# A hybrid decoder trunk whose program is ordered by the list scheduler's time-line model instead of its default model

## The chip, the cores and the metric

The kernel runs on one core of one Trainium2 chip. The metric is device time in microseconds (us), lower is better. Two numbers are used throughout: the time of a run, and the span of one profiled execution, from its first instruction to its last. A core has five engines that work side by side: PE (TensorE, matmuls and transposes; PEld is its weight load), DVE (VectorE), ACT (ScalarE), POOL (GpSimd) and SP (SyncE, which here only issues DMAs). Each engine takes its instructions strictly in the order in which the program lists them for that engine, and waits at semaphores for the others. So the order of the list, engine by engine, is part of the program.

## The reference

The input is x, 1024 tokens of 1024 channels, float32, and two layers of weights. One layer computes, in the reference's own words cut short:

```python
h = rmsnorm(x, norm_gain)
proj = h @ w_in          # split into gq,gk,gv,gb,ga,gz, mq,mkv,mkr,mz, lx,lz
o_a = rmsnorm(gated_delta_rule(q, k, v, g, beta), gdn_out_norm) * silu(gz)  # 4 heads
o_b = causal_block_attention(qf, kf, vm) * silu(mz)                         # 8 heads
o_c = rg_lru(causal_dwconv(lx) + b, ...) * silu(lz)                         # 512 channels
x = x + concat([o_a, o_b, o_c]) @ w_out
```

q, k and v of the first mixer go through a width-4 causal convolution and SiLU. The gated delta rule runs in 16 chunks of 64 tokens, and each chunk needs the state S that the one before it left:

```python
v_new = u_n - w_n @ state
o = (q_n * exp(g_n)) @ state + a_n @ v_new
state = state * exp(g_last) + k_scaled.T @ v_new
```

u_n and w_n come from the inverse of a unit lower triangular 64x64 matrix for each chunk and head. After the second layer a last RMS norm follows.

## The kernel before, in words

**Layout.** Everything is kept transposed: 128 channels on the partitions, 1024 tokens along the row. Every large product is done as three matmuls on a split of both operands into a coarse half and a rest (`mm3`, lines 121 to 123: hi times hi, lo times hi, hi times lo). `load_w` brings one 128-column block of weights: line 104 is the DMA into `wst`, line 109 (ACT) or 111 (DVE) casts it to `whi`, line 112 (POOL) subtracts to get `wlo`.

**The filler.** `in_tile` computes one 128-channel tile of the input projection: 48 matmuls of 512 columns into a two-bank PSUM buffer called `pbig`. There are two such buffers, so the third tile in a row waits until somebody has read the first one out. One layer has 38 such tiles. Names in the listings below carry the tile's number: `pbig_2519` is one tile.

**The chain.** The delta rule handles its four heads as two pairs, "pair 0" and "pair 1", one after the other in each layer. For each pair:

- `gdn_tok` and `gdn_pre` (lines 313 to 367) make the small matrices; the last matmuls are line 367.
- `gdn_inverse` sends the matrices through DRAM into another shape (lines 383, 393, 394) and inverts all of them at once with 60 dependent DVE instructions, `itmp<-inv` and `inv<-inv,itmp`, and one COPY (line 391).
- `gdn_prep`, once for each quarter q of the tokens, loads the inverse back (lines 401 and 403, tiles `mt` and `tq`) and runs four groups of matmuls (lines 415, 421, 426, 434) with DVE steps between them (`z`, `tf`).
- `gdn_scan`, also by quarters, runs the 16 steps of the recurrence. A step is: line 459 on PE (four 128-column matmuls, `pssc<-S,wq`), `vn` on DVE, line 463 on PE (`pssc<-vn,kd`), and the new state `S` on DVE (two instructions), which the next step's line 459 reads. Every second step adds line 471 (`pspr<-vn,at`) for the output.
- `gdn_norm` scales and transposes the outputs: squares on ACT, `ms`, 16 scalings of `at` on POOL (line 95), 16 transposes on PE (line 496), four `gzh` on DVE, each with loads and stores of SP.

After pair 1 the RG-LRU mixer (`lru`) takes four tiles of its own (`lx`: `pbig_3924`, `pbig_4020`, `pbig_4116`, `pbig_4212` in the first layer), convolves each into `u` on ACT and DVE, and goes on with gates and a scan along the row. Then come the first half of the output projection (`pspr`, 384 matmuls), the attention of eight heads and the second half of the output projection. Line 797 transposes the attention's weights, lines 808 and 810 multiply them with the values, line 747 makes scores.

**What sets the order.** The Python code only emits instructions with a priority number. A list scheduler then runs over the whole program and a model of the machine: whenever an engine of the model is free, it takes, among the instructions whose inputs the model has ready, the one with the best priority number. The result is one fixed list for each engine. Three things in the code steer it. The tiles' matmuls are emitted with 20000 added to their priority number, so that they come behind everything else that is ready; the instructions that empty a tile's PSUM buffer and that cast weights are emitted with 20000 taken off; and the place in the code at which a tile is emitted gives its base number:

```python
LOW = 20000
with self.prio(self.LOW):       # in in_tile: the 48 matmuls of a tile
with self.prio(-self.LOW):      # in load_w: cast and subtract; also conv, silu, squares
FILL = ((1, 1, 2, 0, 1), (1, 0, 3, 0, 2))   # tiles emitted between the chain's steps
```

So "filler" is not pinned to a place: the scheduler puts tile matmuls wherever its model of the machine sees PE free and nothing of better priority ready. What the model takes an instruction to last therefore decides where the filler lands. The change touches `kernel()` alone, at the line that opens the context in which all instructions are emitted and ordered.

## Time and profile before

| | before |
|---|---|
| runs, us | 2186.76, 2194.24, 2195.37; median 2194.24 |
| profiled execution, us | 2189.71 |
| its span, us | 2187.9 |
| mean granted TensorE clock | 0.985 |
| PE busy | 2079.0 us, 95% of the span |
| DVE, ACT, POOL busy | 1318.7, 881.4, 705.6 us |
| DMA, mean busy share of 16 engines | 31% |

The profile counts an engine as busy while an instruction of it runs; matmuls are pipelined, so the busy time of PE says that something is in flight, not that it goes at its peak. The work between two rows of one kind is better read from the distance of their starts. In the rows of a timeline the first number is the start in us from the beginning of the span, the second the length in us, then come engine, line, operation, output<-inputs, sizes, and in brackets how long the engine had been idle and what released it.

The two layers run the same code; in the first, the scan of pair 0 lies at about 244 to 306 us, the inverse of pair 1 at 365 to 441, the scan of pair 1 at 441 to 502, its norm at 502 to 517, the attention at 716 to 1045.

### The profile page before, as it was taken

To read this page: it belongs to the slowest core of one execution; us is meant where nothing else is said; L and a number is where in the kernel's file an instruction comes from. 1 tells how busy PE (TensorE), PEld (TensorE's weight loads), DVE (VectorE), ACT (ScalarE), POOL (GpSimd) and SP (SyncE) were. 2 spreads that over 40 slices of the span, in tenths; PEclk is the share of its full clock that TensorE was granted. 3 is DMA by queue.
4 is the path that set the end of the run, shared out by engine and by line. 5 is a ranking of instruction groups with operands and counts; after the bars stand their busy time and mean duration, and the time that the engine had idled before them with its cause. 6 is when DMAs were issued, how large, how long until landed. Compare 5 with 4: busy or idle time off the path is not lost. (4 is left out here: it accounts for less than half of the span.)

```text
span 2187.9 us, 28714 instructions
## 1 busy us (share of the span) xinstructions
PE 2079.0 (95%) x10380; PEld 1691.9 (77%) x10380; DVE 1318.7 (60%) x2496; ACT 881.4 (40%) x1788; POOL 705.6 (32%) x712
## 2 busy tenths in 40 slices
PE   7999999999989999999989999999998999999997
PEld 3788877787778788888668888787876778888874
DVE  6546555644751777776665475474458337776766
ACT  5251235134820453544542413531366115554534
POOL 3222322233452333332142213232236333332322
PEclk9999999999999999999999999999999999999999
DMA  4223212322153115244421331134122530335172
GB/s 141 78 79 101 73 44 87 101 92 90 54 181 116 61 31 193 81 146 157 160 88 49 93 101 44 58 103 139 49 80 94 188 102 27 100 124 165 61 233 98
DMA packets 135101, 222.06 MB, mean 101 GB/s; under 512 B 37808, under 2 KB 60336, under 8 KB 134960
## 3 DMA queue, kind: packets, MB, share of 16 engines
q1 hardware_dynamic: 134960, 220.24, 31.1%
q8 instruction: 82, 1.34, 0.3%
q14 instruction: 59, 0.48, 0.1%
HBM read 147.31 MB, written 72.88 MB: 101 GB/s over the span
## 5 line engine op out<-in xcount | busy, mean ns | idle before, releaser
L112 POOL TENSOR_TENSOR wlo<-wst,whi 128x1024 fp32r<-128x1024 f32 (+3 forms) x196 | 316.6, 1616 | 869.4 <-DVE whi L111 317.2
L121 PE MATMUL pbig<-h,whi 128*128 128x512 f32 x1216 | 486.6, 400 | 8.3 <-ACT h L127 5.3
L123 PE MATMUL pbig<-h,wlo 128*128 128x512 f32 x1216 | 485.8, 400 | 4.0 <-POOL wlo L112 4.0
L122 PE MATMUL pbig<-h,whi 128*128 128x512 f32 x1216 | 486.5, 400 | 3.2 <-POOL h L128 1.6
L121 PEld LDWEIGHTS pbig<-h,whi 128*128 128x128 f32 x1216 | 231.7, 191 | 56.6 <-ACT h L127 6.6
L122 PEld LDWEIGHTS pbig<-h,whi 128*128 128x128 f32 x1216 | 231.4, 190 | 52.2 <-DVE h L128 4.4
L123 PEld LDWEIGHTS pbig<-h,wlo 128*128 128x128 f32 x1216 | 231.6, 190 | 51.3 <-POOL wlo L112 5.3
L86 ACT ACTIVATE P<-pS,mx,scq 128x512 f32<-128x512 f32 (+1 forms) x192 | 128.1, 670 | 155.9 <-DVE mx L89 83.0
L111 DVE CAST whi<-wst 128x1024 fp32r<-128x1024 f32 x92 | 77.2, 840 | 154.1 <-PE pbig L122 121.9
L95 POOL TENSOR_SCALAR P<-P,mx 128x128 f32<-128x128 f32 (+6 forms) x112 | 80.7, 721 | 215.9 <-DVE mx L768 132.2
L109 ACT CAST whi<-wst 128x256 fp32r<-128x256 f32 (+2 forms) x104 | 46.2, 446 | 202.7 <-DMA wst<-in_w_uq 110.2
L127 ACT CAST pth<-pstp 128x512 fp32r<-128x512 f32 x192 | 91.0, 478 | 74.8 <-PE pstp L797 74.7
L757 DVE TENSOR_REDUCE mx<-pS 128x1 f32<-128x512 f32 (+1 forms) x192 | 106.4, 554 | 16.4 <-PE pS L751 9.7
L128 DVE TENSOR_TENSOR ptl<-pstp,pth 128x512 fp32r<-128x512 f32 x192 | 104.8, 552 | 15.0 <-ACT pth L127 13.8
L86 ACT ACT_TABLE_LOAD x81 | 103.9, 1283 | 3.0 <-PE pssc L123 0.8
L797 PE MATMUL pstp<-con,P 128*128 128x128 f32 x576 | 98.1, 275 | 5.8 <-DVE P L772 5.0
L92 DVE TENSOR_TENSOR xt<-pspj,xt 128x512 f32<-128x512 f32 x96 | 66.2, 690 | 49.5 <-PE pspj L123 26.6
L797 PEld LDWEIGHTS pstp<-con,P 128*128 128x128 f32 x576 | 71.7, 141 | 25.7 <-DVE P L772 7.3
L121 PE MATMUL pspj<-lh,whi 128*128 128x512 f32 x208 | 84.3, 405 | 6.7 <-DVE k L128 6.0
L123 PE MATMUL pspj<-lh,wlo 128*128 128x512 f32 x208 | 81.7, 393 | 0.5 <-POOL wlo L112 0.5
L808 PE MATMUL pspo<-pth,vh 128*128 128x512 f32 x192 | 79.3, 413 | 2.8 <-ACT pth L127 2.8
L122 PE MATMUL pspj<-ll,whi 128*128 128x512 f32 x208 | 81.6, 392 | 0.0
(268 smaller groups left out, 4542.0 us busy)
## 6 DMA issues: line engine op xcount, KB each, us to landing
wst<-in_w_in SPq DMA_DIRECT2D x76, 512.0 KB, 3.6
x<-xt SPq DMA_DIRECT2D x128, 256.0 KB, 3.4
xt<-x SPq DMA_DIRECT2D x112, 256.0 KB, 3.4
mzd<-z SPq DMA_DIRECT2D x16, 512.0 KB, 3.5
wst<-in_w_o SPq DMA_DIRECT2D x16, 512.0 KB, 3.6
mz<-mzd SPq DMA_DIRECT2D x32, 256.0 KB, 3.0
wst<-in_w_o SPq DMA_DIRECT2D x64, 128.0 KB, 2.1
xk<-x SPq DMA_DIRECT2D x32, 256.0 KB, 4.1
```

The costliest lines, as they stand in the source:

```text
L86: self.nc.scalar.activation(out, in_, func, **kw)
L95: self.nc.gpsimd.tensor_scalar(out, a, s, 1.0, ALU.mult, ALU.mult)
L111: nc.vector.tensor_copy(hi[:, :n], st[:, :n])
L112: (eng or nc.gpsimd).tensor_tensor(lo[:, :n], st[:, :n], hi[:, :n].bitcast(F32), ALU.subtract)
L121: nc.tensor.matmul(out, ah, bh, start=(j == 0), stop=False)
L122: nc.tensor.matmul(out, ah, bl, start=False, stop=False)
L123: nc.tensor.matmul(out, al, bh, start=False, stop=(j == n - 1))
L127: self.nc.scalar.copy(hi, x)
L128: (eng or self.nc.vector).tensor_tensor(lo, x, hi.bitcast(F32), ALU.subtract)
L757: nc.vector.tensor_reduce(mx[:, j : j + 1], S[j], AX.X, ALU.max, negate=True)
L797: nc.tensor.transpose(tp[:, qi * 128 : qi * 128 + 128], P[qi][:, kb * 128 : kb * 128 + 128], self.ident)
L808: nc.tensor.matmul(po[:, w], vh[:, vs], th[:, w], start=(j == 0), stop=False)
```

## The change

`TileContext` is given one more argument. With it the list scheduler asks another model of the machine, its time-line model, when an instruction would be ready and how long it takes. The statements that emit instructions, their number, their shapes, buffers and priorities stay as they are. The order of the instructions on each engine changes, and with it where the semaphore waits stand.

```diff
-    with tile.TileContext(nc) as tc:
+    with tile.TileContext(nc, schedule_with_timeline_sim=True) as tc:
         Trunk(tc, ins, {"y": out}).build()
```

The listings below show three places, all on PE and all in the first layer; the second layer reads the same. x2, x4 and x16 at the end of a row count the same instruction in a row.

**The scan of pair 0.** On PE before, in the middle of the scan (line 459 and 463 are the two halves of a step, `pbig` is filler, 415 and 421 belong to the next quarter's prep):

```order
L463 MATMUL pssc<-vn,kd 128x128 x2
L471 MATMUL pspr<-vn,at 128x128 x2
L121 MATMUL pbig<-h,whi 128x512
L459 MATMUL pssc<-S,wq 128x128 x2
L122 MATMUL pbig<-h,whi 128x512
L123 MATMUL pbig<-h,wlo 128x512
L121 MATMUL pbig<-h,whi 128x512
L122 MATMUL pbig<-h,whi 128x512
L463 MATMUL pssc<-vn,kd 128x128 x2
L123 MATMUL pbig<-h,wlo 128x512
```

And PE of the change, from the scan's second step on:

```order
L459 MATMUL pssc<-S,wq 128x128 x2
L123 MATMUL pbig<-h,wlo 128x512
L463 MATMUL pssc<-vn,kd 128x128 x2
L471 MATMUL pspr<-vn,at 128x128 x2
L459 MATMUL pssc<-S,wq 128x128 x2
L463 MATMUL pssc<-vn,kd 128x128 x2
L459 MATMUL pssc<-S,wq 128x128 x2
L463 MATMUL pssc<-vn,kd 128x128 x2
L471 MATMUL pspr<-vn,at 128x128 x2
L415 MATMUL pspr<-tq,mt 128x128 x4
L459 MATMUL pssc<-S,wq 128x128 x2
```

Before, three or four filler matmuls stand between the halves of every step. In the change 22 and 21 of them stand in the first step, one in the second, and none in the 14 steps after it. In the scan of pair 1 the first half of the steps have about 22 fillers each between their halves, and the last nine steps none.

**From the matrices to the inverse, pair 1.** PE before, around the last matmuls of line 367 (named by `pspr_2705`) and the two matmuls of line 191 that follow:

```order
L367 MATMUL pspr_2705<-wq_2250,kT_1583 128x128
L367 MATMUL pspr_2705<-wq_2407,kT_1798 128x128
L122 MATMUL pbig_2872<-h_115,whi_2868 128x512
L191 MATMUL pspr_2849<-sq_2570,ep_70 128x512
L191 MATMUL pspr_2853<-sq_2570,ep_70 128x512
L123 MATMUL pbig_2872<-h_107,wlo_2869 128x512
```

PE of the change, at the same place:

```order
L367 MATMUL pspr_2705<-wq_2250,kT_1583 128x128
L367 MATMUL pspr_2705<-wq_2407,kT_1798 128x128
L191 MATMUL pspr_2849<-sq_2570,ep_70 128x512
L191 MATMUL pspr_2853<-sq_2570,ep_70 128x512
L121 MATMUL pbig_3145<-h_101,whi_3141 128x512
```

From there to the first line 415, which needs the inverse, PE has 306 filler matmuls before and 156 in the change: the tiles `pbig_2872` and `pbig_2932` are already done when line 367 ends.

**The norm of pair 1.** PE before, after the last line 471 of pair 1 (32 rows of lx tiles stand between it and the first of these):

```order
L123 MATMUL pbig<-h,wlo 128x512
L496 MATMUL pspr<-con,at 128x128 x8
L121 MATMUL pbig<-h,whi 128x512
L122 MATMUL pbig<-h,whi 128x512
L496 MATMUL pspr<-con,at 128x128 x4
L123 MATMUL pbig<-h,wlo 128x512
L121 MATMUL pbig<-h,whi 128x512
L496 MATMUL pspr<-con,at 128x128 x4
```

PE of the change:

```order
L459 MATMUL pssc<-S,wq 128x128 x2
L463 MATMUL pssc<-vn,kd 128x128 x2
L471 MATMUL pspr<-vn,at 128x128 x2
L496 MATMUL pspr<-con,at 128x128 x16
L121 MATMUL pbig<-h,whi 128x512
L122 MATMUL pbig<-h,whi 128x512
```

The first two lx tiles have moved ahead into the scan, so line 496 follows the scan at once, and the filler behind it is the third lx tile, `pbig_4116`, which needs the buffer that `pbig_3924` holds. On DVE, in both kernels, the convolution that empties `pbig_3924` stands behind the four `gzh` of the norm; in the change it is interleaved with that of `pbig_4020`:

```order
L92 TENSOR_TENSOR ms<-ms,rq 128x16
L89 SCALAR_TENSOR_TENSOR gzh<-pspr,onh,gzh 128x512 x4
L939 TENSOR_SCALAR onh<-par 128x1
L89 SCALAR_TENSOR_TENSOR u<-pbig,par,u 128x1023 x2
L89 SCALAR_TENSOR_TENSOR u<-pbig,par,u 128x1022 x2
L89 SCALAR_TENSOR_TENSOR u<-pbig,par,u 128x1021 x2
```

## The prediction, made before the change was run

> **What bounds the kernel now.** I began with the page's first two parts: who is busy, and at which clock.
>
> ```profile
> span 2187.9 us, 28714 instructions
> PE 2079.0 (95%) x10380; PEld 1691.9 (77%) x10380; DVE 1318.7 (60%) x2496; ACT 881.4 (40%) x1788; POOL 705.6 (32%) x712
> PEclk9999999999999999999999999999999999999999
> ```
>
> PE is busy 2079.0 of 2187.9 us, at nearly full clock. It bounds the kernel, and an order can only change the 108.9 us in which PE has nothing in flight, plus the gaps that busy time hides. The second view, PE's waits summed over the run, says where the small ones are; these are its three largest.
>
> ```profile
> PE pspr L121 <- ACT oh L127: 8.0, 2, 4.0
> PE psst L191 <- DVE sq L177: 7.5, 4, 5.7
> PE pspo L810 <- DVE ptl L128: 6.6, 8, 1.5
> ```
>
> No single wait is large. The third view, PE's busy time by stretches of the first layer, shows how that is reached (columns: stretch, its length, PE busy, clock, DMA share, GB/s).
>
> ```profile
> 244.00:306.00 62.00, 61.05 (x377) 1.00 0.12 39
> 365.00:441.00 76.00, 74.69 (x340) 1.00 0.34 106
> 441.00:502.00 61.00, 60.21 (x372) 0.97 0.25 80
> 502.00:517.00 15.00, 14.82 (x65) 1.00 0.41 136
> 716.00:1045.00 329.00, 317.93 (x1726) 1.00 0.35 112
> 1045.00:1133.00 88.00, 78.38 (x323) 0.94 0.38 132
> ```
>
> The first four are the scan of pair 0, the inverse of pair 1, the scan of pair 1 and its norm. In each of them a chain of dependent steps runs over PE, DVE, ACT, POOL and DRAM, and PE idles 1.0, 1.3, 0.8 and 0.2 us, because filler of the input projection stands between the steps. The last two, attention and what follows, idle 11.1 and 9.6 us. So the question for any new order is whether the filler still stands where the chain leaves PE free. The listings answer it: in all four places it does not.
>
> **The scans.** One step of pair 0's scan in the timeline, PE and DVE rows alone; the number behind the start is the length.
>
> ```profile
> 282.09 0.61 PE L459 MATMUL pssc<-S,wq 128*128 128x128 f32 x4
> 282.45 0.48 PE L122 MATMUL pbig<-h,whi 128*128 128x512 f32 x1
> 282.74 0.42 DVE L92 TENSOR_TENSOR vn<-uu,pssc 64x256 f32<-64x256 f32 x1 [2.28 <-PE pssc L459]
> 283.33 0.71 PE L463 MATMUL pssc<-vn,kd 64*128 64x128 f32 x4
> 283.97 0.71 PE L471 MATMUL pspr<-vn,at 128*128 128x128 f32 x4
> 284.07 0.60 DVE L89 SCALAR_TENSOR_TENSOR S<-S,ge,pssc 128x128 f32<-128x128 f32 x2 [0.91 <-PE pssc L463]
> 284.44 0.48 PE L122 MATMUL pbig<-h,whi 128*128 128x512 f32 x1
> 284.75 0.61 PE L459 MATMUL pssc<-S,wq 128*128 128x128 f32 x4
> 285.43 0.40 PE L121 MATMUL pbig<-h,whi 128*128 128x512 f32 x1
> 285.66 0.39 PE L122 MATMUL pbig<-h,whi 128*128 128x512 f32 x1
> ```
>
> The chain goes 282.09 (459), 282.74 (`vn`), 283.33 (463), 284.07 (`S`), 284.75 (459): 2.66 us. DVE waited for PE both times and PE's 463 for DVE, so this is about what a step costs with no filler at all. PE's own share is 0.36 for line 459 (to the next start, 282.45), 0.64 for 463 and half of the 0.47 for 471 (it comes every second step): 1.24 us. The rest, 1.42 us, is the hole that filler fills, one matmul per 0.23 us (285.43 to 285.66).
>
> A prep between the steps stretches them. On DVE:
>
> ```profile
> 274.39 0.42 DVE L92 TENSOR_TENSOR vn<-uu,pssc 64x256 f32<-64x256 f32 x1 [0.74 <-PE pssc L459]
> 277.87 0.40 DVE L92 TENSOR_TENSOR vn<-uu,pssc 64x256 f32<-64x256 f32 x1
> ```
>
> From 274.39 to 282.74 are two steps with one prep: 8.35 us against 2 x 2.66 = 5.32, so a prep adds 3.0. Its PE work is four groups of eight matmuls at 0.12 (471's pace): 3.8 us.
>
> *Pair 0:* 15 steps without filler and two preps in them: 15 x 2.66 + 2 x 3.0 = 45.9 us, with 15 x 1.24 + 2 x 3.8 = 26 us of PE work, so PE stands about 20 us. The 43 fillers bunched in the first step are not lost, only done earlier than needed. Less the 1.0 of before: **+19 us**. *Pair 1:* nine steps and one prep: 26.9 us, 15 of PE work, **+11 us**. The steps ahead of these carry 22 fillers per half, 5 us where the hole is under 1, so there PE bounds and nothing stands.
>
> Each of these holds as long as a bare step isn't shorter than 2.66. Were it the lengths alone (0.61 + 0.42 + 0.71 + 0.60 = 2.34), the two terms would be 15 and 8; the upper end is in the rivals.
>
> **The inverse of pair 1.** Rows of the timeline for both pairs, and the landing time of `tq`:
>
> ```profile
> 182.04 0.86 DVE L92 TENSOR_TENSOR itmp<-inv 64x30 f32<-64x30 f32 x1
> 203.91 2.41 POOL L112 TENSOR_TENSOR wlo<-wst,whi 128x1024 fp32r<-128x1024 f32 x1 [9.71 <-DVE whi L111]
> 204.05 2.43 DVE L92 TENSOR_TENSOR itmp<-inv 64x150 f32<-64x150 f32 x1
> 210.37 0.18 DVE L92 TENSOR_TENSOR inv<-inv,itmp 64x30 f32<-64x30 f32 x1
> ...
> 363.12 0.69 DVE L92 TENSOR_TENSOR at<-pspr,et 128x512 f32<-128x512 f32 x1 [0.80 <-PE pspr L367]
> 377.70 0.20 DVE L92 TENSOR_TENSOR itmp<-inv 64x30 f32<-64x30 f32 x1
> 412.51 1.12 DVE L391 COPY inv<-inv 64x1024 f32<-64x1024 f32 x1
> 419.98 0.36 SPq L403 DMA_DIRECT2D tq<-dz  x1
> DMA to landing us min/median/max: 2.9/3.8/5.3
> ```
>
> From the end of line 367 to a usable `tq` the chain is: 363.12 to 377.70 (the last `at`, then the latent norm that stands ahead of the inverse on DVE in both orders), 14.6; the inverse, 28.5 by pair 0's rows (182.04 to 210.55; pair 1's 34.8 held more of other tiles' work, and the change has one cast in it); COPY to the issue of `tq`, 7.5; landing, 2.9 at least. Sum 53.5. The filler behind line 367 is 156 matmuls at 0.23 and the two long ones of line 191, about 37.4 us; before it was 306, 70 us, and covered the chain. **+16 us.** Some of it will show ahead of line 415: of the 156 the last twelve belong to `pbig_3444`, whose buffer is emptied on DVE by an instruction that the order puts behind the inverse, and one cast of weights stands between the inverse's own instructions.
>
> The bound below: at 204.05 an `itmp` took 2.43 us, as long as POOL's subtraction beside it, where its neighbours take 0.3. Pair 0's inverse had three such subtractions and two `z` in it; without them it lasts some 22 us, and the term is 10. Above: pair 1's 34.8, and 22. The Trainium skill, "SBUF — State Buffer", in its part on contention at the engine ports, has it that VectorE with two inputs in SBUF and GpSimd take turns at a shared port pair, each holding it for a whole instruction; the row agrees. By it, fewer subtractions during the inverse make it shorter, which speaks for the lower end.
>
> **The norm of pair 1.**
>
> ```profile
> 501.15 0.71 PE L471 MATMUL pspr<-vn,at 128*128 128x128 f32 x4
> 508.59 5.57 POOL L95 TENSOR_SCALAR at<-at,ms 128x128 f32<-128x128 f32 x16 [1.57 <-DVE ms L92]
> 519.62 0.74 DVE L89 SCALAR_TENSOR_TENSOR gzh<-pspr,onh,gzh 128x512 f32<-128x512 f32 x1
> 520.47 3.91 DVE L89 SCALAR_TENSOR_TENSOR u<-pbig,par,u 128x1023 f32<-128x1023 f32 x3
> ```
>
> From the scan's last 471 (end 501.86) to the end of the convolution that frees `pbig_3924` (524.38) pass 22.5 us: squares and `ms`, the scalings on POOL, the stores and loads of the last two `gzh`, the convolution. Before, PE had 21 us of lx tiles to do meanwhile. In the change both are done in the scan, and PE has the 16 transposes, 16 x 0.12 = 1.9 us, before it stands at `pbig_4116`. Two tiles interleaved on DVE add two instructions of 1.3 (3.91 / 3); a gate of ACT and DVE that stood in the chain before may save 2. So 23 - 2 = 21, less what before lost: **+19 us** (12 if `ms` and the DMAs of `gzh` go a third faster without other work beside them, 23 if nothing is saved).
>
> **The clock.** A third of a window without work costs half speed in the next (windows of 3.41 us, PE busy, clock):
>
> ```profile
> 344.51:347.92 3.41, 1.21 (x8) 0.99 0.00 0
> 347.92:351.33 3.41, 3.41 (x12) 0.51 0.23 82
> ```
>
> Busy 0.35 of the window, then 0.51 of the clock for one window: 1.7 us lost. The holes at the inverse and the norm, 16 and 21 us, bring one or two such windows each: **+5 us** per layer.
>
> **What gets better.** In the attention the change puts more PE work between the transposes of line 797 and the line 810 that uses them (median 2.9 to 5.0 us, summed over the order at the rates above). The waits it can take away are those of `pspo L810` (6.6 in both layers) and its neighbours; the attention's idle time is 11.1 us per layer, of which I take half: **-5**. Other stretches (start of a layer, RG-LRU, the matrices of pair 0) have small differences of both signs; I take **-7** per layer, between 0 and the idle time of 15 they hold. The last wait of the run, a column sum, has six matmuls for ten behind it: -2 once. The inverse of pair 0 keeps 57 us of filler for about 54 us of chain: 0, at most +5.
>
> **Sum.** Per layer 19 + 16 + 11 + 19 + 5 - 5 - 7 = 58; two layers less 2: +114. Against the profiled execution, 2189.7, that is 2304. The median of the runs, 2194.2, lies 4.5 above that execution, with runs from 2186.8 to 2195.4; I forecast **2305 us**, slower by 5%.
>
> **The rivals.**
>
> *Faster: the new order wins elsewhere, and the chain shrinks with its cover.* Without filler in DVE's and POOL's way the norm, the inverse and the steps might go as fast as PE's own work, and the rest of the program, 49 us of idle per layer outside the four places, lose half: 2189.7 - 2 x 24 = about 2142, or 2170 with a third of the four terms left. For it: the inverse is stretched by POOL. Against: DVE rows at 282.74 and 284.07 show a chain that already waited for nothing but PE. It decides once a bare step costs under 1.6 us. 8%.
>
> *No change, 2190 to 2200.* Work is conserved: filler done early is not done later, and PE is at 95%. That holds only where every hole still gets something; with 14 steps in a row without filler it must have moved the work to places where PE was already full. It would need losses and gains to cancel within 11 us. 5%.
>
> *Slower still: the clock halves in the bare scans.* Bare steps keep PE busy 1.24 of 2.66 us, 0.47, and the window above was halved after 0.35. If 0.47 is too little, 459 and 463 take 0.7 us more per step: 24 steps and three preps, 20 us per layer, 2345 in all. 15%. The Trainium skill, "TensorE: Matmul & The Clock Gate", in its section on HAM oscillation, puts the rule as no idle gap over about 3.4 us; a bare step has none over 0.7, so by that rule the clock stays full and the sum is 2305. The row above, at 0.35, does not reach up to 0.47, so both stay open.
>
> *The change does nothing.* Excluded by the listings: the orders differ from the first rows on.
>
> **How the numbers follow.** The forecast's own case has 72%: low ends 15, 10, 8, 12 and 2 with gains of 20 give 27 per layer, 2240; high ends 22, 22, 13, 23 and 7 with gains of 5 give 82, 2355. The third rival lies inside that range, the first two outside it with 13%. So the range is 2235 to 2360. Anything under 0.5% (11 us) can't be told from no change here. Slower 0.87, same 0.05, faster 0.08.
>
> **What would show it.** In the profile of the change: PE busy in the two scans down to half over some 46 and 27 us, with 459 every 2.66 us and no `pbig` rows; waits of PE for `vn` and `S` (a few us before, not among the largest) at the top of its list; 14 to 20 us without PE work ahead of pair 1's first line 415, part of it as waits for `whi` or `z`; about 20 us between the transposes of line 496 and `pbig_4116`; the clock at 0.5 in a window or two behind each. Wrong if steps without filler take under 2 us, if the gap ahead of `pbig_4116` is under 10, or if the attention, 329 us, comes out shorter by more than 15.

## The result, and the profile after

The change takes 2328.06 us (median of four runs, 2327.49 to 2343.71) against 2194.8 before: 1.0617 times as long, 95% interval 1.0587 to 1.0647. It is slower by 6.2%; 2305 was forecast.

The first rows of the page, to be held against those of before:

```profile
span 2325.7 us, 28817 instructions
PE 2121.6 (91%) x10380; PEld 1744.6 (75%) x10380; DVE 1314.5 (57%) x2496; ACT 881.5 (38%) x1786; POOL 709.9 (31%) x712
PEclk8999979898899999999999999789969999999998
```

The work is the same, and DVE, ACT and POOL are busy as long as before. PE's 43 us more are not more work: the clock row has dips that before did not show, and a matmul lasts longer at half clock. PE's waits, the largest first (columns: what waited and for what, us in total, times, longest):

```profile
PE pbig L121 <- ACT sq L86: 24.7, 4, 11.2
PE pssc L463 <- DVE vn L92: 23.5, 42, 1.3
PE pbig L121 <- DVE u L89: 21.0, 2, 10.9
PE psst L191 <- DVE sq L177: 18.0, 5, 6.0
PE pspr L496 <- POOL at L95: 10.4, 2, 5.2
PE pssc L459 <- DVE S L89: 9.6, 18, 0.5
```

Before, no wait was over 8.0 us. Five of these six are new and belong to the four places of the prediction: `vn` and `S` to the scans, `at` and `u` to the norm of pair 1, the squares `sq` of ACT to the stretch of the inverse. The sixth, `psst`, lies in the first 30 us of the run. PE's busy time by stretches shows them in place (first layer; stretch, length, busy, clock, DMA share, GB/s):

```profile
274.80:289.50 14.70, 14.70 (x85) 1.00 0.23 71
289.50:341.10 51.60, 40.95 (x219) 0.77 0.06 16
406.80:459.30 52.50, 40.70 (x164) 0.87 0.38 120
477.00:545.75 68.75, 68.22 (x363) 1.00 0.20 66
545.75:575.00 29.25, 22.78 (x124) 0.79 0.06 18
575.00:598.00 23.00, 6.91 (x20) 0.50 0.36 114
794.70:1145.80 351.10, 339.77 (x1843) 0.99 0.36 118
```

The first row is the first step of pair 0's scan with its 43 fillers, the second its 15 bare steps: 51.6 us, and the mean clock is 0.77. The third is the inverse of pair 1. The fourth and fifth are the two halves of pair 1's scan, the sixth its norm up to the third lx tile, the last the attention.

Busy time hides part of a hole, so the table counts in another way: the time between the first or last rows of two lines, less the matmuls between them at the pace of undisturbed rows (0.228 us for 512 columns, 0.112 for a pass of 128). What is left is stall. First layer, in us; the second reads within 3 us of it in every row:

| from, to | before: time, work, stall | change: time, work, stall | more |
|---|---|---|---|
| matrices, pair 0 (first 313 to last 367) | 36.6, 33.7, 2.8 | 62.6, 62.5, 0.1 | -2.7 |
| inverse, pair 0 (to first 415) | 73.6, 74.0, -0.4 | 61.5, 56.9, 4.7 | +5.1 |
| prep and scan, pair 0 (to last 471) | 67.2, 59.1, 8.1 | 86.8, 57.5, 29.4 | +21.3 |
| norm, pair 0 (to first 313 of pair 1) | 22.2, 18.5, 3.7 | 21.5, 16.4, 5.1 | +1.4 |
| matrices, pair 1 | 35.5, 29.4, 6.2 | 44.2, 36.0, 8.2 | +2.0 |
| inverse, pair 1 | 73.4, 71.8, 1.6 | 52.5, 37.4, 15.1 | +13.5 |
| prep and scan, pair 1 | 65.5, 56.0, 9.5 | 115.4, 96.8, 18.5 | +9.0 |
| norm, RG-LRU, first projection (to the first scores) | 225.8, 202.3, 23.5 | 220.1, 176.9, 43.1 | +19.6 |
| attention (to its last 810) | 350.3, 325.8, 24.5 | 351.1, 329.0, 22.1 | -2.4 |

The sum of the last column is 67 us, and the layer ends 68 us later. The columns of work show how the filler moved. The matrices of pair 0 got 29 us more of it than before, and saved 2.7 us of stall with it. The two inverses have 17 and 34 us less, and the stretch from the norm of pair 1 to the scores 25 us less. The prep and scan of pair 0 kept nearly all of their work and lost by its place: more of it stands ahead of the first step, and the rest in that step, ahead of the 15 bare ones. The scan of pair 1 even has 41 us more, in steps where PE was already full.

**A bare step.** PE in the first scan, rows of the timeline, and two windows of 3.41 us there, the step in which the granted clock changes in these traces:

```profile
318.94 0.71 PE L463 MATMUL pssc<-vn,kd 64*128 64x128 f32 x4 [0.52 <-DVE vn L92]
320.18 0.68 PE L459 MATMUL pssc<-S,wq 128*128 128x128 f32 x4
322.63 0.68 PE L459 MATMUL pssc<-S,wq 128*128 128x128 f32 x4 [0.53 <-DVE S L89]
325.97 1.06 PE L459 MATMUL pssc<-S,wq 128*128 128x128 f32 x4
329.35 1.19 PE L459 MATMUL pssc<-S,wq 128*128 128x128 f32 x4 [0.53 <-DVE S L89]
```

```profile
320.50:323.91 3.41, 1.84 (x13) 1.00 0.00 0
323.91:327.32 3.41, 3.12 (x12) 0.50 0.00 0
```

From 320.18 to 322.63 is a step at full clock, 2.45 us; from 325.97 to 329.35 one at half clock, 3.38. The matmuls of line 459 last 0.68 and 1.19. PE idled at most about half a microsecond at a time, was busy 0.54 of the window, and the clock of the next was 0.5. In the whole run 251 us lie in windows at half clock, 65 before. The busy share alone does not decide it: from 1975.90 to 1979.31 PE was busy 1.74 of 3.41 us, and the next window had the full clock. What decides stays open.

**The norm of pair 1:**

```profile
579.86 5.60 POOL L95 TENSOR_SCALAR at<-at,ms 128x128 f32<-128x128 f32 x16 [30.68 <-DVE ms L92]
580.29 5.70 PE L496 MATMUL pspr<-con,at 128*128 128x128 f32 x16 [5.21 <-POOL at L95]
589.84 0.75 DVE L89 SCALAR_TENSOR_TENSOR gzh<-pspr,onh,gzh 128x512 f32<-128x512 f32 x1 [0.78 <-DMA gzh<-gzd]
590.70 7.22 DVE L89 SCALAR_TENSOR_TENSOR u<-pbig,par,u 128x1023 f32<-128x1023 f32 x6
596.88 0.77 PE L121 MATMUL pbig<-h,whi 128*128 128x512 f32 x1 [10.89 <-DVE u L89]
```

The scan's last 471 is at 574.66, the third lx tile starts at 596.88: 22 us for 16 transposes, as the order read. It is two holes and not one: PE waits 5.2 us for POOL's scalings, ahead of the transposes, and 10.9 for the convolution, which stands behind `gzh`.

**The inverse of pair 1:**

```profile
407.01 2.01 PE L191 MATMUL pspr<-sq,ep 128*128 128x512 f32 x4
407.15 0.69 DVE L92 TENSOR_TENSOR at<-pspr,et 128x512 f32<-128x512 f32 x1 [0.29 <-PE pspr L367]
413.33 0.16 DVE L92 TENSOR_TENSOR itmp<-inv 64x30 f32<-64x30 f32 x1
420.25 0.79 PE L121 MATMUL pbig<-h,whi 128*128 128x512 f32 x1 [11.23 <-ACT sq L86]
422.96 2.37 POOL L177 TENSOR_TENSOR sq<-sq 128x1024 f32<-128x1024 f32 x1 [21.89 <-DVE inv L92]
423.00 2.55 DVE L92 TENSOR_TENSOR itmp<-inv 64x198 f32<-64x198 f32 x1
446.93 1.12 DVE L391 COPY inv<-inv 64x1024 f32<-64x1024 f32 x1
459.26 1.13 PE L415 MATMUL pspr<-tq,mt 128*128 128x128 f32 x8 [0.57 <-DMA tq<-dz]
```

The chain from line 367 through the inverse to `tq` takes 52.5 us (53.5 forecast). But the hole isn't where it was looked for: PE stands 11.2 us right at the start, at a tile that needs the buffer of the first mq tile, which ACT can square only when the latent norm (of `mkv`) on DVE has given back its buffers.

### The profile page after: what moved, and what is told of

Read it like the earlier page. It is cut to its first block, busy times and chain, and to the rows that moved or that the text cites. A ratio compares the mean times of both kernels' runs of the same rounds, so it can differ in the third digit from the quotient of the medians.

```text
span 2325.7 us, 28817 instructions
## 1 busy us (share of the span) xinstructions
PE 2121.6 (91%) x10380; PEld 1744.6 (75%) x10380; DVE 1314.5 (57%) x2496; ACT 881.5 (38%) x1786; POOL 709.9 (31%) x712
## 5 line engine op out<-in xcount | busy, mean ns | idle before, releaser
L112 POOL TENSOR_TENSOR wlo<-wst,whi 128x1024 fp32r<-128x1024 f32 (+3 forms) x196 | 321.9, 1643 | 917.8 <-DVE whi L111 346.3
L121 PEld LDWEIGHTS pbig<-h,whi 128*128 128x128 f32 x1216 | 234.6, 193 | 108.7 <-ACT sq L86 26.7
L122 PEld LDWEIGHTS pbig<-h,whi 128*128 128x128 f32 x1216 | 235.1, 193 | 53.2 <-DVE h L128 4.7
L123 PEld LDWEIGHTS pbig<-h,wlo 128*128 128x128 f32 x1216 | 234.9, 193 | 52.6 <-POOL wlo L112 3.3
L121 PE MATMUL pspj<-lh,whi 128*128 128x512 f32 x208 | 86.3, 415 | 11.2 <-DVE k L128 6.6
L89 DVE SCALAR_TENSOR_TENSOR S<-S,ge,pssc 128x128 f32<-128x128 f32 x128 | 38.7, 344 | 85.8 <-PE pssc L463 85.5
```

The lines of the kernel that those rows point to most:

```text
L112: (eng or nc.gpsimd).tensor_tensor(lo[:, :n], st[:, :n], hi[:, :n].bitcast(F32), ALU.subtract)
L121: nc.tensor.matmul(out, ah, bh, start=(j == 0), stop=False)
L122: nc.tensor.matmul(out, ah, bl, start=False, stop=False)
L123: nc.tensor.matmul(out, al, bh, start=False, stop=(j == n - 1))
```

## The experiments

The kernels differ from the two originals in order alone, but where a diff shows more. They are made with edges of order: the program is traced and ordered once, PE's list is taken (and edited), and in a second tracing each PE instruction gets an edge of order, without a wait, from the one ahead of it in the list. Names of instructions are the same in both tracings. The change itself was timed in the first round only; the median of before was 2194.8 us there and 2195.0 to 2198.9 in the later rounds, so a difference from the change is sure to about 4 us. The core of it, in `kernel()`:

```diff
+    _, rec, o = emit((PE,), schedule_with_timeline_sim=True)   # rec: names by tile, scan step, ...
+    pe = o[PE]                                                # PE's list, then edited
+    nc, _, _ = emit(want=[pe], schedule_with_timeline_sim=True)
+            for p, q in zip(order, order[1:]):                # inside emit
+                tc.add_manual_dep(traced[q], p, DependencyInfo(NoSync, DATA), reason="order")
```

### Whose order is it: PE's or the others'

```diff
 pe_before:
+    _, _, o = emit((PE,))                                     # PE as the default model has it
+    nc, _, _ = emit(want=[o[PE]], schedule_with_timeline_sim=True)
 pe_after:
+    _, _, o = emit((PE,), schedule_with_timeline_sim=True)    # PE as the time-line model has it
+    nc, _, _ = emit(want=[o[PE]])
```

> The time-line model orders DVE, ACT, POOL and SP, but PE keeps the order it had before (edges of order only, no waits added). Theory: the loss sits in PE's own order, in the holes of the four places, so it goes away: 2190 to 2215 us, and both scans show filler between their steps again. Rival: the loss comes from the order of DVE and ACT (evacuations behind the inverse, convolutions interleaved): then it stays above 2280.

> The other half: the default model orders DVE, ACT, POOL and SP, PE is tied to the order that the time-line model gave it. Theory: PE's order alone brings the loss: 2310 to 2340 us, bare scans at 2.4 us a step as in the change. Rival (the other engines' order): 2190 to 2220.

Measured: with PE's list of before 2237.9 us, 1.0185 [1.0163, 1.0207] of before; with PE's list of the change 2397.1, 1.0905 [1.0876, 1.0934]. Both missed the expected numbers, both upwards. The first part of the theory holds: with PE's old list the four places are as before (stall of the scans 7.7 and 8.9 us, of the second inverse -0.3, line 471 to the last 496 of pair 1 1.0). But 41 us remain (against 2197.3, the median of before in these runs), and they are new ones. PE's largest waits in that kernel:

```profile
PE pS L747 <- ACT P L86: 14.9, 14, 3.6
PE pspo L810 <- DVE ptl L128: 14.1, 15, 2.1
PE pbig L122 <- DVE h L128: 13.4, 2, 7.0
```

The attention stalls 38.8 us there, where both original kernels stall 22 to 25. And the change's list of PE with the default order on the other engines is worse than the change:

```profile
PE pspr L415 <- DMA tq<-dz: 58.0, 4, 16.7
```

In the change that wait is 8.6. The default order on DVE makes both inverses' stretches longer. For pair 0 more of the tiles' work stands between the inverse's instructions (the inverse takes 55.8 us for 45.0 in the change, the stretch 74.9 for 61.5). For pair 1 the latent norm stands ahead of the inverse (14.8 us from line 367 to its first instruction, 6.6 in the change), and the stretch takes 64.2 us for 52.5. So an order is good or bad as a set: 200 us for PE's list alone and 41 for the other engines' alone add up to far more than the 133 of both together.

### Undoing the four places in the change, one by one

```diff
 spread_scan0:  # the fillers of pair 0's scan, one or two behind each 459 and 463
+    fill = [n for n in part if n in filler]
+    gaps = [rec[k, l, 0, s][-1] for s in range(16) for k in ("459", "463")]
 lx_back:       # first two lx tiles behind the last 471, transposes between them
+    pe[at:at] = lx[:33] + pt[0] + pt[1] + lx[33:41] + pt[2] + lx[41:49] + pt[3] + lx[49:]
 mq1_back:      # tile pbig_2932 from the matrices of pair 1 to behind its line 191
+    at = pe.index(rec["tile", l, MT_MQ + 2][0]); pe[at:at] = rec["tile", l, MT_MQ + 1]
```

> The change, with one part of PE's order undone: in the scan of pair 0 the 46 filler matmuls that stand in its first two steps are dealt out over all 16 steps, in both layers. Theory: the first step falls from 14.7 us to a common one, 16 steps and three preps take about 50 us in place of 66 with 39 us of PE work in them, so the stall falls from 27 to about 11: 16 us per layer, 2328 - 33 = about 2295. Rival: the steps wait for something else than filler could cover (POOL's scalings, the loads of the preps), then no more than 5 us per layer: above 2315.

Measured 2309.3 us, 1.0508 [1.0485, 1.0531]: 19 us less than the change, 33 had been expected. From the first 459 to the last 471 it took 52.6 us for 66.3, the stall fell from 27.7 to 14.0. The steps look as they should:

```profile
308.82 0.61 PE L459 MATMUL pssc<-S,wq 128*128 128x128 f32 x4
309.18 0.48 PE L122 MATMUL pbig<-h,whi 128*128 128x512 f32 x1
309.50 0.40 PE L123 MATMUL pbig<-h,wlo 128*128 128x512 f32 x1
309.94 0.71 PE L463 MATMUL pssc<-vn,kd 64*128 64x128 f32 x4
311.36 0.61 PE L459 MATMUL pssc<-S,wq 128*128 128x128 f32 x4
```

A step is 2.54 us and stays at full clock, but three fillers don't fill it. What is missing is filler as such: 44 matmuls in this scan (the 46 of the expectation were miscounted by two), where before has 104.

> The change, with another part undone: the first two lx tiles (96 matmuls, 22 us) are taken out of the scan of pair 1 and put behind its last line 471, around the transposes of the norm, in both layers. Theory: the first seven steps of that scan are bound by PE with 22 fillers in each half and lose nothing, the 20 us hole between line 496 and the third lx tile is filled: 17 to 20 us per layer, 2328 - 36 = about 2292. Rival: the norm's chain only moves the same wait behind the lx tiles (its DMAs and the convolutions are what is late): no more than 10 us per layer, above 2308.

Measured 2296.73 us, 1.0449 [1.0424, 1.0473], 31 us less than the change; 36 expected, the rival (above 2308) is out. From the scan's end to the first scores the stall fell from 43.1 to 22.5 us. The scan that gave the tiles up stalls 7 us more (25.8 for 18.5): its fillers now end in the third step and not the seventh. That had not been counted.

> The change, with one tile of the filler moved in PE's order of both layers: pbig_2932 (48 matmuls, 11 us) from between the steps of pair 1's matrices to behind the two line 191 that follow its last line 367. In the trace of the change PE stood 11.2 us there, at a tile whose buffer ACT had not emptied. Theory: the matrices of pair 1 get by with less filler (26.6 us there, 21.6 of them PE work; the chain of a quarter takes about 5 us by itself), the chain through the inverse starts 5 to 6 us earlier, and the moved tile covers the 11 us: 5 us per layer, 2328 - 10 = about 2318. Rival: the matrices' chain is as slow without the filler, and nothing is won: 2325 to 2330.

Measured 2348.24 us, 1.0673 [1.065, 1.0695]: slower than the change, so both were wrong. The matrices did get 3.6 us shorter, but the stretch behind them grew from 52.5 to 58.8. DVE and POOL there:

```profile
408.74 0.20 DVE L92 TENSOR_TENSOR itmp<-inv 64x30 f32<-64x30 f32 x1 [0.73 <-DMA inv<-dn]
416.44 2.55 POOL L112 TENSOR_TENSOR wlo<-wst,whi 128x1024 fp32r<-128x1024 f32 x1 [26.96 <-DVE itmp L92]
416.76 2.39 DVE L92 TENSOR_TENSOR itmp<-inv 64x150 f32<-64x150 f32 x1
448.04 1.11 DVE L391 COPY inv<-inv 64x1024 f32<-64x1024 f32 x1
```

The inverse starts 4.6 us earlier than in the change and ends 1.1 later. More tiles are worked on during it, so five subtractions or sums of POOL lie inside it and not three, each holding one of its 0.3 us instructions for 2.4, besides two more casts and a `z` on DVE. That POOL and DVE exclude each other there is seen in the rows; it is the rule of the Trainium skill, "SBUF — State Buffer", section "Who interferes with whom", on the shared port pair of VectorE and GpSimd, and the traces agree. Filler that covers the inverse also lengthens it.

That is the smaller part of the loss: matrices and inverse together are 2.7 us longer in the first layer. The prep and scan behind them took 121.0 us for 115.4, with 25 us at half clock for 12; the second layer reads the same. Why more of its windows fell to half clock, no run shows.

> The change with PE's order as it is, but five in place of four of the 128x1024 buffers that phase A shares (tag c4), so that ACT can write out and square the first mq tile without waiting for the latent norm on DVE. In the change PE stands 11.2 us for that tile's squares, right behind pair 1's last line 367. Theory: the stretch from line 367 to the first line 415 is as long as its chain through the inverse and DRAM (52 us in the change), not as the waits inside it: the 11 us get shorter and PE waits at line 415 instead; 2322 to 2334. Rival: the buffer is what costs there: 6 to 8 us per layer, 2312 to 2317.

```diff
 c4_five:  # PE's list of the change
-        return self.pa.tile([128, T], F32, name=name, tag="c4", bufs=4)
+        return self.pa.tile([128, T], F32, name=name, tag="c4", bufs=5)
```

Measured 2338.87 us, 1.0656 [1.0632, 1.068]. The fifth buffer halved the wait for ACT, and the rest moved behind, as the theory said:

```profile
410.43 0.80 PE L121 MATMUL pbig<-h,whi 128*128 128x512 f32 x1 [5.58 <-ACT sq L86]
459.06 2.08 PE L415 MATMUL pspr<-tq,mt 128*128 128x128 f32 x8 [11.56 <-DMA tq<-dz]
```

The stretch is as long as its chain, now 56.5 us, 4 more than in the change. The trace shows where. From line 367 to the inverse's first instruction DVE needs 8.5 us for 6.6: ACT, which now has a buffer, writes out the mq tile (1.1 us) between the two `rb` that DVE waits for, and more of the latent norm comes ahead of the inverse. The inverse takes 35.7 us for 33.6, with four of POOL's operations in it and not three. Why the time came out above the expected range is not shown in full: in the first layer the prep and scan behind took 121.0 us for 115.4, again with 25 us at half clock for 12, in the second 117.8 for 116.4.

> The change, with the four places of PE's order undone together, in both layers: the fillers of each scan dealt out over its 16 steps, the first two lx tiles behind the scan of pair 1, pbig_2932 behind the line 191; DVE, ACT, POOL and SP as the time-line model then orders them. Theory: the holes are independent, and each gives what it gave alone: 19 for the first scan, 31 for lx, 10 for pbig_2932, and 14 to 20 for the second scan, whose stall lx_back had raised from 18.5 to 26: 2240 to 2255. Rival: the fillers that are left don't reach, and a hole that is closed opens another: above 2275.

```diff
 undo_all:  # the three edits above, and the fillers of both scans dealt out over their steps
+        deal(l, 0)
+        deal(l, 1)
```

Measured 2245.8 us, 1.0208 [1.0191, 1.0226]: 82 of the 133 us are gone, by moving matmuls in PE's list alone. The stalls, first layer: 14.4 for the first scan, 10.1 at the second inverse, 7.5 for the second scan, 18.3 from the norm to the scores (27.7, 15.1, 18.5 and 43.1 in the change). The matrices of pair 1, which gave up a tile, stall 7 us more than in the change. Against before, some 25 us per layer are left: about 9 at these matrices, 8 each at the first scan and the second inverse, 5 at the first inverse, less 5 behind the norm.

### Doing one part alone, in the kernel before

```diff
 before_lx:       # default model on all engines; PE's list edited
+        at = pe.index(rec["471", l, 1, 7][0]); pe[at:at] = lx      # first two lx tiles, and the rest of the tile ahead of them
 before_bunched:
+        pe[a : b + 1] = [n for n in part if n in filler] + [n for n in part if n not in filler]
```

> The kernel before with its own scheduler, and one part of the change alone: in PE's order of both layers the first two lx tiles stand ahead of the last line 471 of pair 1 instead of around the transposes of the norm. Theory: that alone makes the hole between line 496 and the third lx tile, as in the change, where the stretch from the scan's end to the first scores lost 20 us per layer more than before: 17 to 20 us per layer, 2197 + 37 = about 2234. Rival: the hole needs the time-line model's order on the other engines too: below 2212.

Measured 2246.99 us, 1.0226 [1.0204, 1.0248]. The part alone costs 49 us, 37 had been expected. The default scheduler then interleaves the two convolutions on DVE as the change has it. The stall from the scan's end to the scores goes from 23.5 to 51.0 us in the first layer. The hole has the same place and cause, but another instruction stands in it: PE waits 11.9 us at the first gate of the RG-LRU, for `uh`, which comes of the convolution, and not at the third lx tile.

> The kernel before, and another part alone: all filler that stands in the scan of pair 0 is put into its first step, ahead of the first line 463, in both layers; the 15 steps behind it are bare. Theory: 27 us of filler at once, then 16 steps at 2.4 us and three preps at 3.0, 47 us, and some 6 more where the granted clock goes to 0.5, in place of 60: 20 us per layer, 2197 + 40 = about 2237. Rival: more than that, above 2255, if the bunched tiles also run out of weights or of PSUM buffers ahead of the first step.

Measured 2250.19 us, 1.0249 [1.0222, 1.0276]: 52 us more, 40 had been expected. First 459 to last 471 takes 80.9 us for 60.3, that is 20.6 more, and 20.6 in the second layer. With 1.8 more at the norm behind it in one layer and 3.4 in the other that is about 46 of the 52 measured. The bunched tiles did not run out of anything: the work ahead of the bare steps went through at full pace.

### The clock

```diff
 warm_scan:  # ahead of 459 and of 463 in each bare step, into unused columns
+        self.note(self.nc.tensor.matmul(p[:, 256:512], self.ident, self.con[:, 0:256], start=True, stop=True))
```

> The change, with two matmuls that do nothing useful (256 columns, into unused columns of the step's own PSUM banks) in each step without filler, ahead of line 459 and of line 463; everything else in the change's order. In the change a bare step takes 2.4 us at full clock, and 3.4 to 3.9 once the granted clock is at 0.5, as in the last five steps of the first scan. Theory: it is the clock that makes these steps longer, PE kept busier stays at full clock, and steps stay under 2.8: 5 to 8 us per layer, 2312 to 2320. Rival: the steps would be long anyway, or the added matmuls stand in the chain's way: 2328 or more.

Measured 2318.22 us, 1.0534 [1.0509, 1.0558], within the range of the theory. PE by windows over 23.5 us of the scan, then two steps of it (line 1089 is the added matmul):

```profile
314.00:337.50 23.50, 21.77 (x133) 1.00 0.00 1
```

```profile
323.75 0.72 PE L459 MATMUL pssc<-S,wq 128*128 128x128 f32 x4
324.31 0.60 PE L1089 MATMUL pssc<-con 128*128 128x256 f32 x2
326.61 0.61 PE L459 MATMUL pssc<-S,wq 128*128 128x128 f32 x4
```

The clock stays at 1.0, and no step without a prep is over 2.9 us, although PE has more to do. In the change the same steps took up to 3.9. The first scan is 5.3 and 4.4 us shorter in the two layers, the second 2.5 and 2.8. So the clock costs the change some 15 us in the scans, of which about 10 reach the end.

### Two attempts at a faster kernel

```diff
 hybrid:       # all five engines tied: before's lists, the attention's instructions in the change's order
+        want.append([n if part[n] is None else next(mine[part[n]]) for n in first[e]])
 warm_before:  # before's lists on all five engines, and matmuls without a use ahead of five waits
+    WARM["out", l, 1] = 9, ("out", l, 0), 21     # and four more such places
```

> Both orders in one kernel: on all five engines the order of before, but within the attention and the second half of the output projection the order that the time-line model gave. In the two traces that stretch stalled 24.5 us before and 22.1 in the change, per layer. Theory: an order is good as a whole, over all engines, so the stretch keeps its gain: 2 to 3 us per layer, 2185 to 2195 against 2197. Rival: as with PE's order alone, the seams cost more than the stretch wins: above 2205.

Measured 2198.19 us, 0.9996 [0.9976, 1.0016]: no difference is seen. The interval reaches from 5 us faster to 4 slower, so a gain as small as the one expected, 4 to 6 us in both layers, is not surely out. In the traces, one execution each, the attention stalls 24.2 and 22.2 us; before has 24.5 and 23.9, the change 22.1 and 22.4. The second layer has the gain and the first has not, so whether the order of that stretch carries it stays open.

> The kernel before with its own order on all five engines, and matmuls without a use (256 columns, into PSUM banks that the next useful matmul overwrites) at five places where PE stood for 1 to 4 us and the granted clock was 0.5 in the window after: ahead of the second line 360 of pair 1 (5 of them), the gates of the last lx tile (2), the oh blocks of the first output projection (9), the first line 808 of the last head (3), and the first tile of the second layer (4). Theory: what the warmed scan showed holds here: eight to ten windows at half clock less, up to 1.7 us each where PE has work to do in them: 2197 - 8 to 17 = 2180 to 2189, the fastest version so far. Rival: the windows at half clock lie in stretches that wait for other engines anyway, and the added matmuls cost what they win: 2192 to 2202.

Measured 2202.93 us, 1.0018 [1.0004, 1.0032]: nothing won, rather a little lost. Windows at half clock fell from 65 to 50 us in the profiled run. Up to the first scores it was 4.5 us ahead of before, but the attention then took 354.7 us for 350.3, and 356.1 for 349.6 in the second layer. Whether the added matmuls do that, or chance, is left open.

## Why the prediction was right, and where its sizes were off

**The sign and the mechanism** held: PE's list has four places in each layer where a chain is left bare, and by the table they are 62 of the 67 us of stall in the first layer (scan of pair 0 without its prep 19.7, inverse 13.5, scan of pair 1 without its prep 9.3, norm to scores 19.6). Undoing them in PE's list alone takes back 82 of 133 us; two of them done alone in the kernel before cost 49 and 52 us.

**The scans**, forecast 19 and 11 us: 19.7 and 9.3 more stall. The sum came out by two errors that cancel. A bare step at full clock is 2.45 us and not the 2.66 that the prediction took from a step with three fillers. And some of the steps, the last five of the first scan among them, ran at half clock, 3.4 to 3.9 us each. So that the term fits is luck, and the third rival, the clock in the bare scans, came true in part: the prediction gave it 15% and 20 us per layer. The warmed scan puts it at 7 to 8 per layer in the scans. The row that the prediction read as "a third of a window without work" has PE busy for 1.21 of 3.41 us, that is without work for two thirds of it.

**The inverse of pair 1**, forecast 16: 13.5 more than before, and the chain 52.5 us against 53.5. That the chain's sum fits is luck, for its terms do not. The prediction had the latent norm ahead of the inverse on DVE in both orders, and 14.6 us up to the inverse's first instruction. In the change it is 6.2 us (407.15 to 413.33), because most of the latent norm stands between the inverse's own instructions. The inverse then took 33.6 us (413.33 to 446.93) and not 28.5, with the rest of that norm and three of POOL's operations in it. From the COPY to line 415 it was 12.3 us and not 10.4. That PE would wait ahead of line 415, in part for `whi` or `z`, was wrong: it stood 11.2 us at the first mq tile's buffer. With a fifth buffer the wait moved to line 415, so the size was set by the chain, as forecast, and the place by the buffer.

**The norm of pair 1**, forecast 19 and, with the half clock behind it, up to 24: 19.6 from the scan's end to the scores. `lx_back` and `before_lx` confirm the cause from both sides. One sign came close to failing: the gap ahead of `pbig_4116` was to be about 20 us, and under 10 would have been wrong. It was 10.9 and 10.1 us in the two layers, since the other part of the hole lies ahead of the transposes. Nor did the half clock behind it last a window or two: it began in the scan's bare steps and lasted 37.5 us.

**What was mis-sized** is the term "what gets better" and what stood at nothing beside it. The attention gave 2.4 and 1.5 us per layer, not 5. "Other stretches, -7" came to -2.7 for the matrices of pair 0, +2.0 for those of pair 1 and, in the two layers, +1.4 and +3.0 for the first norm. The inverse of pair 0, forecast "0, at most +5", cost 5.1 and 4.7: its instructions took 45.0 us and not 28.5, since convolutions of other tiles and four of POOL's operations stood between them. Over two layers these are some 33 us more than forecast. Against that stand the clock's own term, 10 (what the clock cost lies inside the holes as counted here), and about 6 by which the second inverse and the second scan came out smaller. The preps and the norm of pair 1 add 4, and the 2 of the last wait did not go. That makes the 23 by which the forecast was short. The step that failed is that gains were taken from waits that could go, without a row that showed them going.

**The rivals.** "Work is conserved" and "faster elsewhere" are out by the total. Whether it would be enough to look at PE's list was the prediction's silent assumption: it was, for this change, but only since the other engines' lists went with it; `pe_before` and `pe_after` show 41 and 200 us when they don't.

## What to carry to other kernels

Where filler from a limited stock covers several chains, look in the new order for the places where a chain is left bare, and price each as chain time less the work that stands in it; a run of steps without filler is read from the list, before anything is timed. Price bare steps at both clocks if PE is busy for about half of them. The lists of the engines belong together: to take one engine's order from one schedule and the rest from another can cost more than either schedule. Read the other engines' lists inside the chain, too: the inverse of pair 0, the same 61 instructions, took 28.5 us before, 45.0 in the change and 55.8 in `pe_after`, by what stood between them.

## What was unexpected

- The granted clock fell to 0.5 behind a window in which PE was busy 1.84 of 3.41 us and idle never much over 0.5 us at a time. The Trainium skill, "TensorE: Matmul & The Clock Gate", in its section on HAM oscillation, names idle gaps over about 3.4 us as what to avoid; by that rule the bare scans would have stayed at full clock, and the measurement says otherwise.
- Matmuls without a use that keep the clock up gained about 10 us in the bare scans, where the slow matmuls sit on the chain; at five waits of the kernel before they gained nothing.
- One more tile under cover of the inverse made the inverse's stretch 6 us longer: POOL's work for the tiles holds up DVE, and their casts stand between the inverse's instructions.
